# First token block of a PEER router: gates by accumulating indirect transfers instead of matmuls

## The chip, the cores and the metric
The kernel runs on one core of one Trainium2 chip. The metric is device time in microseconds (us) of one execution, the median of several. One execution was also run under the hardware profiler; the rows below come from that one. Two timings of this kernel that differ by less than about 0.2% can't be told apart.

## The reference
512 tokens of width 1024 pass through two layers. Each layer is a mixer (layer 0: pooling and retention; layer 1: a gated linear recurrence), a layer norm, a PEER block and a second layer norm. The change is in the PEER block, which both layers run with their own weights:

```python
q = (xt @ w_q).reshape(T, 8, 2, 128)                  # 8 heads, two half queries each
s = einsum('thpd,hpkd->thpk', q, sub_keys)            # 128 scores for each half
s_top, i_top = top_k(s, 16)
cand = s_top[:, :, 0, :, None] + s_top[:, :, 1, None, :]
best, pos = top_k(cand, 16)                           # 16 experts of 16384 for each head
eid = i_top[..., 0] * 128 + i_top[..., 1]             # at pos
gate = softmax(best)
act = gelu(einsum('td,thkd->thk', xt, u_tab[eid]))
out = einsum('thk,thkd->td', gate * act, v_tab[eid])
```

So every token uses 8 x 16 = 128 of 16384 experts, each with a gate.

## The kernel before
Tokens are cut into four blocks of 128 (`tb` 0 to 3). Blocks 0 to 2 (`TD` = 384 tokens) are computed **densely**: all 16384 experts are multiplied out for all 384 tokens, and a dense table of gates, nearly all zeros, is multiplied in between. Block 3 is computed **sparsely**: 256 indirect loads on POOL's queue (the engine is GpSimd) fetch the rows it needs.

The 16384 experts are 128 chunks of 128, in 32 groups of four (`NG` = 32, `NB` = 4). For one chunk `mm1` does 24 matmuls of 384 columns (three products of split float32 for each of 8 slices of the width), then Gelu; I call this a **lookahead block** where it is done early. `mm2` multiplies the gated result with the chunk of `peer_v` and adds it up in PSUM over all chunks. Weights pass through `stream`: a load on SP's queue into one of 5 `raw` buffers, ACT rounds it to `hi`, DVE (VectorE) subtracts to get `lo`; there are 6 `hi` and 6 `lo` buffers.

The **route** of a layer runs ahead of the experts:
- `route_topk`, first half: for each of four chunks `c` of the query projection (two heads each), 96 matmuls of 512 columns, then for each token block the scores against the keys on PE and the best 16 of 128 on DVE.
- `route_topk`, second half: for each token block (order 3, 0, 1, 2), all 8 heads at once: add the candidates, take the best 16, softmax, and `lookup`, which turns positions into the two key numbers of each expert. For blocks 0 to 2 the numbers and gates are transposed by PE into `kT`.
- `route_gates`: for every 8 dense tokens one **gate round**: DVE builds two one-hot tables `oh` and `og`, PE multiplies them in 16 matmuls of 128 columns in float16 (half of them on line 779, half on 780), ACT copies the product to `gbuf`. Every 32 tokens, `gbuf` (2 MB) is written to the DRAM tensor `gd`. There are 48 rounds a layer.

The route is a Python generator that yields an estimated cost at several places (`YC`, `Y2`, and constants). `peer` adds these up, and for each 2.8 units it emits one lookahead block. So there are 14 groups (`NLA`), 56 blocks, computed during the route and, all but two groups, spilled to DRAM `sp`. A scheduler then fixes the order on each engine; each engine runs its own in order.

In `experts`, SP loads the gates of a group (`gt` from `gd`) and, for the early groups, `ge` from `sp`; DVE multiplies; PE does `mm2` and the `mm1` of the other 18 groups. Beside it POOL fetches rows for block 3 (`gather_rounds`, line 832).

Of the kernel before, what the change touches and what calls it, by code (L numbers as in the profile page):

```python
# [20 lines left out]
P = 128  # L21
# [7 lines left out]
GS = 16384.0  # L29
NB = 4  # L30
NG = NE // NB
TD = 3 * P
NSD = TD // 32
NLA = 14
KEEP = 2
# [3 lines left out]
Y2 = 1.4  # L39
# [4 lines left out]
GW = 8  # L44
WINDOWS = (2, 4, 8, 16)
NEG = -3.0e38


class Kern:
# [547 lines left out]
    def peer(self, layer, xT, hs, out):  # L597
        nc, tc, io = self.nc, self.tc, self.io
        gd = self.dram.tile([NG, P, NSD, NB, 32], F32, name="gd%d" % layer, tag="gd%d" % layer)
        sp = self.dram.tile([NLA, P, NB, TD], F32, name="sp%d" % layer, tag="sp%d" % layer)  # L600
        with tc.tile_pool(name="pe", bufs=1) as pe:
            self.pe = pe
            self.eid = pe.tile([P, P], I32, name="eid", tag="eid")
            self.gate3 = pe.tile([P, P], F32, name="gate3", tag="gate3")
            self.x3 = pe.tile([P, D], F32, name="x3", tag="x3")
            g, b = self.load_ln(layer, 0)

            def norm(tb):
                self.layernorm(tb, hs[tb], g, b, xT)
                if tb == NTB - 1:  # L610
                    nc.scalar.copy(self.x3, hs[tb])
                    nc.scalar.mul(hs[tb], hs[tb], ALPHA)

            self.out_proj(io["c_w_out" if layer else "ab_w_out"], xT, hs, norm)
            self.kept = {}
            look = self.lookahead(layer, xT, sp)
            with tc.tile_pool(name="rk", bufs=1) as rk:
                kT = rk.tile([P, TD // GW, 4, GW], F16, name="kT", tag="kT")
# [4 lines left out]
                for gen in (self.route_topk(layer, xT, kT), self.route_gates(layer, kT, iot, gd)):  # L623
# [8 lines left out]
            self.experts(layer, xT, hs, gd, sp, lambda tb: self.layernorm(  # L632
                tb, hs[tb], g1, b1, None if layer else xT, out if layer else None))
        return xT
# [23 lines left out]
    def route_topk(self, layer, xT, kT):  # L658
        nc, tc, io = self.nc, self.tc, self.io
        with tc.tile_pool(name="rt", bufs=1) as rt, tc.tile_pool(name="rt2", bufs=2) as rt2, \  # L660
                tc.tile_pool(name="rs2", bufs=1) as rs2:
            i16 = rt.tile([P, 16], F16, name="i16", tag="i16")
# [7 lines left out]
            def sink_q(n, ps):  # L670
                q = rt2.tile([P, T], F32, name="qh", tag="qh", bufs=5)
                nc.scalar.copy(q, ps)
                qs.append(q)

# [25 lines left out]

            for tb in (3, 0, 1, 2):
                sv = stop[:, tb].rearrange("p (h two) s -> p h two s", two=2)
                s0, s1 = sv[:, :, 0, :], sv[:, :, 1, :]
                iv = itop[:, tb].rearrange("p (h two) s -> p h two s", two=2)
                i0, i1 = iv[:, :, 0, :], iv[:, :, 1, :]
                cand = rs2.tile([P, 8, 64], F32, name="cand", tag="cand")
                at = 0
                for a, b, m in ((0, 1, 16), (1, 4, 8), (4, 8, 4), (8, 16, 1)):
                    n = b - a
                    ov = cand[:, :, at:at + n * m].rearrange("p h (i j) -> p h i j", j=m)  # L710
                    nc.vector.tensor_tensor(ov, s0[:, :, a:b, None].broadcast_to([P, 8, n, m]),
                                            s1[:, :, None, 0:m].broadcast_to([P, 8, n, m]), ALU.add)
                    at += n * m
                best = rs2.tile([P, 8, 16], F32, name="best", tag="best")
                pos = rs2.tile([P, 8, 16], U32, name="pos", tag="pos")
                for h in range(8):
                    c2 = rs2.tile([P, 64], F32, name="c2", tag="c2")
                    cv = cand[:, h, :]
                    nc.vector.max(out=best[:, h, 0:8], in_=cv)
                    nc.vector.max_index(out=pos[:, h, 0:8], in_max=best[:, h, 0:8], in_values=cv)  # L720
                    nc.vector.match_replace(out=c2, in_to_replace=best[:, h, 0:8], in_values=cv, imm_value=NEG)
                    nc.vector.max(out=best[:, h, 8:16], in_=c2)
                    nc.vector.max_index(out=pos[:, h, 8:16], in_max=best[:, h, 8:16], in_values=c2)
                    yield 0.7
                if tb == 3:
                    gate = self.gate3.rearrange("p (h s) -> p h s", h=8)
                else:
                    gate = rs2.tile([P, 8, 16], F32, name="gate", tag="gate")
                nc.vector.tensor_tensor(gate, best, best[:, :, 0:1].broadcast_to([P, 8, 16]), ALU.subtract)
                nc.scalar.activation(gate, gate, AF.Exp)  # L730
                sm = rs2.tile([P, 8], F32, name="gsm", tag="gsm")
                nc.vector.tensor_reduce(sm, gate, AX.X, ALU.add)
                nc.vector.reciprocal(sm, sm)
                nc.vector.tensor_tensor(gate, gate, sm[:, :, None].broadcast_to([P, 8, 16]), ALU.mult)
                kk = yield from self.lookup(rs2, pos, i0, i1, thr, i16)
                if tb == 3:
                    ef = rs2.tile([P, P], F32, name="ef", tag="fi")
                    fl = "p h s -> p (h s)"
                    nc.vector.scalar_tensor_tensor(ef, kk[0].rearrange(fl), 128.0, kk[1].rearrange(fl),
                                                   ALU.mult, ALU.add)  # L740
                    nc.vector.tensor_copy(self.eid, ef)
                    continue
                tg = slice(tb * P // GW, (tb + 1) * P // GW)
                ghT, glT = kT[:, tg, 2, :], kT[:, tg, 3, :]
                pt = self.psC.tile([P, 512], F32, name="pC", tag="pC")
                for i, t in enumerate((kk[0], kk[1], gate)):
                    nc.tensor.transpose(pt[:, i * P:(i + 1) * P], t.rearrange("p h s -> p (h s)"), self.ident)
                nc.scalar.copy(kT[:, tg, 0:2, :].rearrange("p g i w -> p i g w"),
                               pt[:, 0:2 * P].rearrange("p (i g w) -> p i g w", i=2, w=GW))
                gs = rs2.tile([P, P // GW, GW], F32, name="gs", tag="gs")  # L750
                nc.scalar.mul(gs, pt[:, 2 * P:3 * P].rearrange("p (g w) -> p g w", w=GW), GS)
                nc.scalar.copy(ghT, gs)
                nc.vector.tensor_tensor(glT, gs, ghT, ALU.subtract)

    def route_gates(self, layer, kT, iot, gd):
# [3 lines left out]
        with tc.tile_pool(name="rg", bufs=2) as rg:  # L759
            b5 = [P, 2, Q, P, L]  # L760
            for s in range(NSD):
# [25 lines left out]
    def lookup(self, pool, pos, i0, i1, thr, i16):  # L787
        nc = self.nc
        sh, sx = [P, 8, 16], [P, 8, 16, 16]
        pf = pool.tile(sh, F32, name="pf", tag="pf")  # L790
        nc.vector.tensor_copy(pf, pos)
        m = pool.tile(sh, F32, name="m", tag="m")
        m2 = pool.tile(sh, F32, name="m2", tag="m2")
        mi = pool.tile(sh, U32, name="mi", tag="mi")
# [6 lines left out]
        yield 1.5  # L801
        d0 = pool.tile(sh, F16, name="d0", tag="d0")
# [3 lines left out]
        for src, cst, op, val, nm in ((pf, thr, ALU.is_ge, d0, "ka"), (mi, i16, ALU.is_equal, i1, "kb")):  # L806
            x = pool.tile(sx, F16, name="xp", tag="xp", bufs=2)
            nc.scalar.copy(x, src[:, :, :, None].broadcast_to(sx))
            nc.vector.tensor_tensor(x, x, cst[:, None, None, :].broadcast_to(sx), op)
            yield 2.0  # L810
            nc.vector.tensor_tensor(x, x, val[:, :, None, :].broadcast_to(sx), ALU.mult)
            yield 2.0
            t1 = pool.tile([P, 8, 16, 8], F16, name="t1", tag="t1")
            nc.vector.tensor_tensor(t1, x[:, :, :, 0:8], x[:, :, :, 8:16], ALU.add)
            t2 = pool.tile([P, 8, 16, 4], F16, name="t2", tag="t2")
            nc.vector.tensor_tensor(t2, t1[:, :, :, 0:4], t1[:, :, :, 4:8], ALU.add)
            t3 = pool.tile([P, 8, 16, 2], F16, name="t3", tag="t3")
            nc.vector.tensor_tensor(t3, t2[:, :, :, 0:2], t2[:, :, :, 2:4], ALU.add)
            k = pool.tile(sh, F32, name=nm, tag=nm)
            nc.vector.tensor_tensor(k, t3[:, :, :, 0], t3[:, :, :, 1], ALU.add)  # L820
            res.append(k)
            yield 1.0
# [32 lines left out]
    def experts(self, layer, xT, hs, gd, sp, norm):  # L855
        nc, tc, io = self.nc, self.tc, self.io
        with tc.tile_pool(name="ex", bufs=2) as ex, tc.tile_pool(name="ga", bufs=2) as ga:
# [19 lines left out]
            def front(i):  # L877
# [3 lines left out]
                if b == 0:  # L881
# [7 lines left out]
                    nc.sync.dma_start(out=gt, in_=gd[g])  # L889
# [95 lines left out]
def _shape_constants():  # L985
# [24 lines left out]
    c["ident"] = np.eye(P, dtype=f)  # L1010
    return c
# [57 lines left out]
```

## Time and profile before

| | |
|---|---|
| median of 3 runs | 2875.28 us (2873.82 to 2875.84) |
| the profiled execution's own time | 2876.77 us |
| its span in the profile | 2875.0 us |
| busy PE, DVE, ACT, POOL | 99%, 82%, 40%, 25% of the span |
| route of layer 0, first scores to last gate round | 190 to 553 us |
| first `mm2` of layer 0 | 573.89 us |
| DMA, read and written in HBM | 669.31 MB, 71.30 MB |

The span is what the profile's rows cover; the execution's own time is 1.8 us longer. PE is the matmul engine; an engine's busy share is an average over stages. Layer 1 repeats the PEER block of layer 0 some 1482 us later.

### The profile page before, as it was taken

Reading aid. Unit: us, or ns where it says so; the run is one execution under the profiler, and the core shown is the slowest. Engines: PE = TensorE matmul, PEld = TensorE weight load, DVE = VectorE, ACT = ScalarE, POOL = GpSimd, SP = SyncE. Lnnn points to the kernel's source line nnn. Section 1 sums busy time; section 2 is a strip of 40 time slices with the busy share of each in tenths; the row PEclk is TensorE's granted clock in tenths of the full one; section 3 lists DMA queues with packets and bytes.
Section 4 is the critical chain, followed back from the end, with each engine's and each line's share of the span. In section 5 each row is a group of like instructions: output and inputs, shape, how many; then the busy total and the mean of one; then the engine's idle time right before and its main releaser. Section 6 shows DMA issues by size and latency. Waiting matters only on the chain.

```text
span 2875.0 us, 42578 instructions
## 1 busy us (share of the span) xinstructions
PE 2858.8 (99%) x15832; PEld 2556.3 (89%) x15832; DVE 2369.7 (82%) x4482; ACT 1143.7 (40%) x1707; POOL 722.6 (25%) x539
## 2 busy tenths in 40 slices
PE   9999999999999999999999999999999999999998
PEld 7888999988898888888888889999888989889887
DVE  6779999788888888876797779999678888888786
ACT  3333565433333333334334333565433333333332
POOL 0000000145444455440000000000244454544440
PEclk9999999999999999999999999999999999999999
DMA  6223469999999999995322234479998999989982
GB/s 223 91 97 114 149 206 287 280 368 373 351 345 365 340 376 340 343 363 166 104 81 70 96 99 137 157 244 281 316 375 335 361 371 340 371 331 350 353 323 74
DMA packets 283792, 743.41 MB, mean 259 GB/s; under 512 B 21696, under 2 KB 120512, under 8 KB 283584
## 3 DMA queue, kind: packets, MB, share of 16 engines
q1 hardware_dynamic: 209856, 472.22, 47.2%
q0 software_dynamic: 73728, 268.47, 24.0%
q8 instruction: 124, 2.03, 0.3%
q14 instruction: 84, 0.69, 0.1%
HBM read 669.31 MB, written 71.30 MB: 258 GB/s over the span
## 4 chain that ended last, share of the span: by engine, by line
PE 93%; DVE 5%; DMA 1%; issue 1%; ACT 0%; POOL 0%; SPq 0%; DVEq 0%
PE pB L937 18%; PE pC L937 18%; PE pA L91 14%; PE pA L93 14%; PE pA L92 14%; PE pC L91 2%; PE pC L93 2%; PE pC L92 2%; PE pB L779 1%; PE pB L780 1%; DVE lo L76 1%; DVE oh L772 1%; DVE og L773 1%; PE pC L158 1%; DVE s L695 1%
## 5 line engine op out<-in xcount | busy, mean ns | idle before, releaser
L75 ACT CAST hi<-raw 128x1024 fp32r<-128x1024 f32 (+1 forms) x609 | 638.1, 1051 | 654.6 <-PE pA L92 412.5
L76 DVE TENSOR_TENSOR lo<-raw,hi 128x1024 fp32r<-128x1024 f32 (+1 forms) x609 | 736.4, 1216 | 178.8 <-ACT hi L75 170.1
L832 POOL DMA_INDIRECT row<-in_u,eid x256 | 388.1, 1516 | 1491.2 <-DVE av L842 581.2
L91 PE MATMUL pA<-xThi,hi 128*128 128x384 f32 (+2 forms) x2032 | 700.8, 345 | 2.4 <-ACT hi L75 2.4
L93 PE MATMUL pA<-xThi,lo 128*128 128x384 f32 (+2 forms) x2032 | 699.6, 344 | 0.0
L92 PE MATMUL pA<-xTlo,hi 128*128 128x384 f32 (+2 forms) x2032 | 697.3, 343 | 0.1
L91 PEld LDWEIGHTS pA<-xThi,hi 128*128 128x128 f32 x2032 | 382.0, 188 | 19.8 <-ACT hi L75 3.3
L92 PEld LDWEIGHTS pA<-xTlo,hi 128*128 128x128 f32 x2032 | 381.9, 188 | 17.0 <-DVE xTlo L76 0.4
L93 PEld LDWEIGHTS pA<-xThi,lo 128*128 128x128 f32 x2032 | 381.7, 188 | 14.3
L75 ACT CAST ch<-ge 128x384 fp32r<-128x384 f32 x256 | 131.4, 515 | 607.0 <-PE pC L937 483.8
L832 POOL DMA_INDIRECT row<-in_v,eid x256 | 327.6, 1280 | 158.6 <-DVE h L851 102.2
L851 DVE SCALAR_TENSOR_TENSOR h<-row,cf,h 128x1024 f32<-128x1024 f32 x256 | 327.7, 1280 | 0.9 <-DMA row<-in_v,eid 0.8
L842 DVE CUSTOM_DVE_ANT_0 row<-row,x 128x1024 f32<-128x1024 f32 x256 | 310.9, 1215 | 3.8 <-DMA row<-in_u,eid 3.8
L937 PE MATMUL pC<-hi,ch 128*128 128x512 f32 x768 | 300.0, 391 | 0.0
L937 PE MATMUL pB<-hi,cl 128*128 128x512 f32 x768 | 299.6, 390 | 0.4 <-DVE cl L76 0.3
L937 PE MATMUL pB<-lo,ch 128*128 128x512 f32 x768 | 299.9, 390 | 0.0
L937 PE MATMUL pB<-hi,ch 128*128 128x512 f32 x768 | 299.1, 389 | 0.7 <-ACT ch L75 0.7
L937 PE MATMUL pC<-hi,cl 128*128 128x512 f32 x768 | 299.5, 390 | 0.0
L937 PE MATMUL pC<-lo,ch 128*128 128x512 f32 x768 | 298.7, 389 | 0.0
L905 DVE TENSOR_TENSOR ge<-ge,gt 128x384 f32<-128x384 f32 x256 | 134.5, 551 | 157.3 <-DMA ge<-sp 146.9
L76 DVE TENSOR_TENSOR cl<-ge,ch 128x384 fp32r<-128x384 f32 x256 | 141.0, 551 | 62.5 <-ACT ch L75 61.9
L937 PEld LDWEIGHTS pB<-hi,cl 128*128 128x128 f32 x768 | 144.1, 188 | 32.1 <-DVE cl L76 1.6
(261 smaller groups left out, 4126.1 us busy)
## 6 DMA issues: line engine op xcount, KB each, us to landing
raw<-in_peer_ut SPq DMA_DIRECT2D x256, 512.0 KB, 4.9
raw<-in_peer_v SPq DMA_DIRECT2D x256, 512.0 KB, 6.9
gd<-gbuf SPq DMA_DIRECT2D x24, 2048.0 KB, 10.0
gt<-gd SPq DMA_DIRECT2D x64, 768.0 KB, 7.2
sp<-ge SPq DMA_DIRECT2D x24, 768.0 KB, 5.3
ge<-sp SPq DMA_DIRECT2D x24, 768.0 KB, 9.4
raw<-in_peer_w_q SPq DMA_DIRECT2D x32, 512.0 KB, 4.3
raw<-in_c_w_in SPq DMA_DIRECT2D x32, 512.0 KB, 3.9
```

The source lines that it names most:

```text
L75: self.nc.scalar.copy(hi, src)
L76: return self.nc.vector.tensor_tensor(lo, src, hi.bitcast(F32), ALU.subtract)
L91: nc.tensor.matmul(ps, ah, bh, start=(first and i == 0), stop=False)
L92: nc.tensor.matmul(ps, ah, bl, start=False, stop=False)
L93: nc.tensor.matmul(ps, al, bh, start=False, stop=(last and i == n - 1))
L158: nc.tensor.transpose(ps[:, i * P:(i + 1) * P], src[:, (q + i) * P:(q + i + 1) * P], self.ident)
L695: nc.vector.match_replace(out=s2, in_to_replace=mx[:, 0:8], in_values=sc, imm_value=NEG)
L832: nc.gpsimd.indirect_dma_start(out=t, out_offset=None, in_=io[name], in_offset=bass.IndirectOffsetOnAxis(ap=self.eid[:, j:j + 1], axis=0))
L842: nc.vector.tensor_tensor_reduce(ur, ur, x3, 1.0, 0.0, ALU.mult, ALU.add, av[:, k:k + 1])
L851: nc.vector.scalar_tensor_tensor(acc, vr, coefs[i // GQ][:, i % GQ:i % GQ + 1], acc, ALU.mult, ALU.add)
L905: nc.vector.tensor_tensor(gv, gv, gt[:, :, b, :], ALU.mult)
L937: nc.tensor.matmul(acc[hf], a[:, ts], b[:, hf * 512:(hf + 1) * 512], start=first and i == 0, stop=last and i == 2)
```

## The change
Block 0 no longer goes through the transposes and gate rounds. After the scores of token block 0 in each chunk, the two heads of that chunk choose their experts at once (`choose(0, c * 2, 2)`), and a new class `Scatter` computes, for each of the 32 (head, rank) columns, the address of each token's gate in a new DRAM tensor `gz`, and issues one indirect transfer per column that **adds** 128 gates of 4 bytes to it. `gz` is filled with zeros first, by 32 transfers of 256 KB on SP's queue. As two heads of a token may choose the same expert, each transfer of a head is made to wait for all 16 of the head before it. `gd` and `kT` lose block 0, so 32 gate rounds a layer are left of 48. In `experts`, `gt` is loaded in two pieces, from `gd` and from `gz`; the `gz` piece of the first two groups goes through POOL's queue. `Y2`, the cost put down for a gate round, goes from 1.4 to 2.0. The number of groups ahead stays 14. `choose` and `lookup` are the old code with the number of heads as an argument.

```diff
 NLA = 14
+NSZ = 4
-Y2 = 1.4
+Y2 = 2.0
+class Scatter:
+    def __init__(self, k, pool, layer):
...
+        self.dst = k.dram.tile([NG, P, NSZ, NB, 32], F32, name=self.name, tag=self.name)
+        z = pool.tile([P, NSZ * NB * 32], F32, name="zero", tag="zero")
+        nc.gpsimd.memset(z, 0.0)
+        for g in range(NG):
+            nc.sync.dma_start(out=self.dst[g].rearrange("p s b t -> p (s b t)"), in_=z)
+    def place(self, k, pool, c, k0, k1):
...
+        nc.vector.tensor_scalar(x, k1, 0.25, -0.375, ALU.mult, ALU.add)
+        nc.vector.tensor_scalar(x, x, RND, RND, ALU.add, ALU.subtract)
+        nc.vector.tensor_scalar(y, k0, float(row), self.pcol, ALU.mult, ALU.add)
+        nc.vector.scalar_tensor_tensor(y, k1, 32.0, y, ALU.mult, ALU.add)
+        nc.vector.scalar_tensor_tensor(y, x, float(P * row - 32 * NB), y, ALU.mult, ALU.add)
+        nc.vector.tensor_copy(idx, y)
+        flat = self.dst.rearrange("g p s b (t o) -> (g p s b t) o", o=1)
+        for h in range(2):
...
+            for j in range(h * 16, h * 16 + 16):
+                d = nc.gpsimd.indirect_dma_start(
+                    out=flat, out_offset=bass.IndirectOffsetOnAxis(ap=idx[:, j:j + 1], axis=0),
+                    in_=gate[:, j:j + 1], in_offset=None, compute_op=ALU.add).ins
+                for p in self.last:
+                    tc.add_manual_dep(d, p.name, LANDED, reason="adds of different heads may meet")
...
+            self.last = head
...
                     yield YC[c]
+                    if tb == 0:
+                        yield from choose(0, c * 2, 2)
+            for tb in (3, 1, 2):
+                yield from choose(tb, 0, 8)
...
-            for s in range(NSD):
+            for s in range(NSD - NSZ):
                 gbuf = rg.tile([P, P, 32], F32, name="gbuf", tag="gbuf")
...
-                    nc.sync.dma_start(out=gt, in_=gd[g])
+                    nc.sync.dma_start(out=gt[:, NSZ:], in_=gd[g])
+                    gz.read(nc.gpsimd if i < 2 * NB else nc.sync, gt[:, :NSZ], g)
```

Three places show how instructions move. The first is DVE's order while token blocks 0 and 1 of the first query chunk are ranked. Before, there is nothing but the ranking of scores (`stop`, `ix`, `s`; lines 693 to 697):

```order
L695 MATCH_REPLACE s_1702<-stop,pB 128x128
L693 MAX stop<-pB 128x8
L696 MAX stop<-s_1702 128x8
L694 MAX_INDEX ix<-stop,pB 128x8
L697 MAX_INDEX ix<-stop,s_1702 128x8
```

Of the changed kernel, the same place (ranking is now lines 806 to 810):

```order
L809 MAX stop<-s_1871 128x8
L750 MAX best<-c_1742 128x8
L810 MAX_INDEX ix<-stop,s_1871 128x8
L751 MAX_INDEX pos<-best,c_1742 128x8
L759 TENSOR_TENSOR gate_1405<-best 128x32
L806 MAX stop<-pB 128x8
L856 CAST pf<-pos 128x32
L807 MAX_INDEX ix<-stop,pB 128x8
L860 TENSOR_SCALAR m<-pf 128x32
L861 TENSOR_SCALAR m_1757<-pf 128x32
```

The choice of two heads stands between the rankings, in instructions a quarter as wide as those of an eight-head choice. The second place is POOL's order from the start of the route of layer 0 to the first row fetched for block 3 (`iot` and `i` are constant tables). Before:

```order
L944 MEMSET z 128x512
L620 ISA
L620 IOTA iot 128x256
L663 IOTA i_1417 128x16
L832 DMA row<-in_u,eid 128x1024 x9
```

Of the changed kernel:

```order
L1010 MEMSET z 128x512
L65 MEMSET zero 128x512
L674 ISA
L674 IOTA iot 128x256
L717 IOTA i_1462 128x16
L86 DMA gz_1415<-gate_1405,idx_1409 2097152x1 x32
L86 DMA gz_1415<-gate_1406,idx_1410 2097152x1 x32
L86 DMA gz_1415<-gate_1407,idx_1411 2097152x1 x32
L86 DMA gz_1415<-gate_1408,idx_1412 2097152x1 x32
L97 DMA gt<-gz_1415 128x512 x2
L897 DMA row<-in_u,eid 128x1024 x9
```

128 adding transfers and two gate loads now stand ahead of POOL's first row. The third place is SP's queue behind the layer norm's constants. Before:

```order
L179 DMA lnb<-in_ln_b 128x1024
L665 DMA thr<-in_thr 128x16
L678 DMA keys<-in_keysT 128x512
L81 DMA raw<-in_peer_w_q 128x1024
L678 DMA keys<-in_keysT 128x512
```

Of the changed kernel:

```order
L62 DMA pcol<-in_pcol 128x1
L67 DMA gz_1415<-zero 128x512 x32
L719 DMA thr<-in_thr 128x16
L791 DMA keys<-in_keysT 128x512
L134 DMA raw<-in_peer_w_q 128x1024 x2
L134 DMA raw<-in_peer_ut 128x1024
```

The zeros now stand ahead of the third load of the query projection's weights.

## Rows read from the trace of the kernel before

**Rows 1.** The page: busy us, share of the span, instructions of an engine
```profile
PE 2858.8 (99%) x15832; PEld 2556.3 (89%) x15832; DVE 2369.7 (82%) x4482; ACT 1143.7 (40%) x1707; POOL 722.6 (25%) x539
```

**Rows 2.** Waits of PE: who for whom, us in total, times, longest
```profile
PE pA L91 <- ACT hi L75: 2.4, 2, 1.9
...
PE pB L684 <- DVE s L695: 0.6, 2, 0.3
```

**Rows 3.** Timeline of PE among gate rounds: start, us, instruction
```profile
458.34 0.42 PE L91 MATMUL pA<-xThi,hi 128*128 128x384 f32 x1
...
464.69 0.42 PE L91 MATMUL pC<-xThi,hi 128*128 128x384 f32 x1
```

**Rows 4.** Timeline of PE among lookahead blocks alone
```profile
300.45 0.34 PE L91 MATMUL pC<-xThi,hi 128*128 128x384 f32 x1
...
304.62 0.34 PE L91 MATMUL pA<-xThi,hi 128*128 128x384 f32 x1
```

**Rows 5.** Timeline of PE around one transpose of chosen experts
```profile
350.38 0.27 PE L747 MATMUL pC<-c_ident,ka 128*128 128x128 f32 x1
...
350.62 0.42 PE L91 MATMUL pC<-xThi,hi 128*128 128x384 f32 x1
350.88 0.33 PE L92 MATMUL pC<-xTlo,hi 128*128 128x384 f32 x1
```

**Rows 6.** First and last scores of layer 0: ns min/median/max, starts
```profile
L684 PE MATMUL pB<-keys,qh x128: 269/275/378, 190.0 to 292.0; 128*128 128x128 f32 x128
```

**Rows 7.** Windows: DVE busy us (instructions), clock, DMA share, GB/s
```profile
293.00:403.00 110.00, 106.02 (x440) 1.00 0.47 157
```

**Rows 8.** Windows: PE, PEld, DVE, ACT, POOL busy us, clock, DMA
```profile
260.00:280.00 20.00, 20.00 (x106) 17.76 (x105) 17.26 (x77) 7.70 (x11) 0.00 (x0) 1.00 0.32 105
```

**Rows 9.** Timeline of DVE: small instructions of the choice of experts
```profile
306.84 0.17 DVE L803 COPY d<-itop 128x8 f16<-128x8 f16 x1
306.90 0.22 DVE L804 TENSOR_TENSOR d<-itop 128x120 f16<-128x120 f16 x1
...
314.72 0.18 DVE L733 RECIPROCAL gsm<-gsm 128x8 f32<-128x8 f32 x1
314.82 0.17 DVE L722 MAX8 best<-c 128x8 f32<-128x64 f32 x1
```

**Rows 10.** The one-hot tables: ns min/median/max, first and last start
```profile
L779 PE MATMUL pB<-og,oh x768: 217/218/235, 407.2 to 2035.6; 128*128 128x128 f16 x192
...
L772 DVE TENSOR_TENSOR oh<-iot,kT x96: 1214/1218/1226, 403.7 to 2030.7; 128x2048 f16<-128x2048 f16 x96
```

**Rows 11.** Softmax's table loads on ACT, 190 to 400 us
```profile
L730 ACT ACT_TABLE_LOAD x4 | 5.1, 1283 | 0.1
```

**Rows 12.** Timeline of POOL, a row fetched early in layer 1
```profile
2052.95 0.93 POOL L832 DMA_INDIRECT row<-in_u,eid  x1 [0.30 <-issue]
```

**Rows 13.** Indirect row loads: ns min/median/max, starts; and landing
```profile
L832 POOL DMA_INDIRECT row<-in_u,eid x256: 933/1679/1968, 565.6 to 2756.9; - x128
L832 POOL DMA_INDIRECT row<-in_v,eid x256: 932/1295/2147, 583.4 to 2790.6; - x128
...
DMA to landing us min/median/max: 4.6/8.3/12.2
```

**Rows 14.** Loads of gates: ns min/median/max, first and last issue
```profile
L889 SPq DMA_DIRECT2D gt<-gd x64: 326/327/877, 564.7 to 2785.9; - x64
```

**Rows 15.** Timeline of SP's issues at the end of layer 0's mixer
```profile
124.59 0.43 SPq L179 DMA_DIRECT2D lnb<-in_ln_b  x1
...
128.49 0.43 SPq L81 DMA_DIRECT2D raw<-in_peer_w_q  x1
```

**Rows 16.** DMA issues: count, KB each, median us to landing
```profile
gd<-gbuf SPq DMA_DIRECT2D x24, 2048.0 KB, 10.0
...
raw<-in_peer_w_q SPq DMA_DIRECT2D x32, 512.0 KB, 4.3
```

**Rows 17.** Timeline of ACT: first cast of a late load
```profile
161.21 1.05 ACT L75 CAST hi<-raw 128x1024 fp32r<-128x1024 f32 x1 [0.78 <-ACT xThi L163]
```

More of the change, by code (lines that the diff above doesn't have):

```diff
@@ L46, with read @@
 NEG = -3.0e38
+RND = 12582912.0
+LANDED = mybir.DependencyInfo(mybir.DependencyClass.Sync, mybir.DependencyReason.DATA)
+class Scatter:
+    def __init__(self, k, pool, layer):
+        nc, self.tc = k.nc, k.tc
+        self.name = "gz%d" % layer
+        self.last = []
+        self.gate = [k.pe.tile([P, 2, 16], F32, name="gate0", tag="gate0", bufs=4) for _ in range(4)]
+        self.idx = [k.pe.tile([P, 2 * 16], I32, name="idx0", tag="idx0", bufs=4) for _ in range(4)]
+        self.pcol = pool.tile([P, 1], F32, name="pcol", tag="pcol")
+        nc.sync.dma_start(out=self.pcol, in_=k.io["pcol"])
+        self.dst = k.dram.tile([NG, P, NSZ, NB, 32], F32, name=self.name, tag=self.name)
[4 more added lines that the diff above has]
+    def place(self, k, pool, c, k0, k1):
+        nc, tc = k.nc, k.tc
+        idx, gate = self.idx[c], self.gate[c].rearrange("p h s -> p (h s)")
+        x = pool.tile([P, P], F32, name="ix0", tag="fi")[:, :32]
+        y = pool.tile([P, P], F32, name="iy0", tag="fj")[:, :32]
+        nc.vector.tensor_scalar(x, k1, 0.25, -0.375, ALU.mult, ALU.add)
+        nc.vector.tensor_scalar(x, x, RND, RND, ALU.add, ALU.subtract)
+        row = NSZ * NB * 32
+        nc.vector.tensor_scalar(y, k0, float(row), self.pcol, ALU.mult, ALU.add)
[4 more added lines that the diff above has]
+        for h in range(2):
+            key = "%s.%d" % (self.name, c * 2 + h)
+            head = []
+            for j in range(h * 16, h * 16 + 16):
[4 more added lines that the diff above has]
+                    tc.add_manual_dep(d, p.name, LANDED, reason="adds of different heads may meet")
+                tc.declare_no_dep(d, group=key, reason="a head's sixteen experts differ")
+                tc.add_to_no_dep_group(key, d)
+                head.append(d)
+            self.last = head
+    def read(self, engine, out, g):
+        d = engine.dma_start(out=out, in_=self.dst[g]).ins
+        for p in self.last:
+            self.tc.add_manual_dep(d, p.name, LANDED, reason="all adds of the last head")
@@ L598, in peer @@
         nc, tc, io = self.nc, self.tc, self.io
-        gd = self.dram.tile([NG, P, NSD, NB, 32], F32, name="gd%d" % layer, tag="gd%d" % layer)
+        gd = self.dram.tile([NG, P, NSD - NSZ, NB, 32], F32, name="gd%d" % layer, tag="gd%d" % layer)
         sp = self.dram.tile([NLA, P, NB, TD], F32, name="sp%d" % layer, tag="sp%d" % layer)
@@ L617, in peer @@
             with tc.tile_pool(name="rk", bufs=1) as rk:
-                kT = rk.tile([P, TD // GW, 4, GW], F16, name="kT", tag="kT")
+                gz = Scatter(self, rk, layer)
+                kT = rk.tile([P, (TD - P) // GW, 4, GW], F16, name="kT", tag="kT")
                 iot = rk.tile([P, P, 2], F16, name="iot", tag="iot")
@@ L622, in peer @@
                 credit = CREDIT0
-                for gen in (self.route_topk(layer, xT, kT), self.route_gates(layer, kT, iot, gd)):
+                for gen in (self.route_topk(layer, xT, kT, gz), self.route_gates(layer, kT, iot, gd)):
                     for cost in gen:
@@ L631, in peer @@
             g1, b1 = self.load_ln(layer, 1)
-            self.experts(layer, xT, hs, gd, sp, lambda tb: self.layernorm(
+            self.experts(layer, xT, hs, gd, gz, sp, lambda tb: self.layernorm(
                 tb, hs[tb], g1, b1, None if layer else xT, out if layer else None))
@@ L656, in lookahead, with route_topk @@
                 yield
-    def route_topk(self, layer, xT, kT):
+    def route_topk(self, layer, xT, kT, gz):
         nc, tc, io = self.nc, self.tc, self.io
@@ L699, in route_topk @@
                     yield YC[c]
[L701 to L753, printed above, removed]
@@ L788, in lookup @@
         nc = self.nc
-        sh, sx = [P, 8, 16], [P, 8, 16, 16]
-        pf = pool.tile(sh, F32, name="pf", tag="pf")
+        n = pos.shape[1]
+        part = n / 8.0
+        sh, sx = [P, 8, 16], [P, n, 16, 16]
+        pf = pool.tile(sh, F32, name="pf", tag="pf")[:, :n]
         nc.vector.tensor_copy(pf, pos)
-        m = pool.tile(sh, F32, name="m", tag="m")
-        m2 = pool.tile(sh, F32, name="m2", tag="m2")
-        mi = pool.tile(sh, U32, name="mi", tag="mi")
+        m = pool.tile(sh, F32, name="m", tag="m")[:, :n]
+        m2 = pool.tile(sh, F32, name="m2", tag="m2")[:, :n]
+        mi = pool.tile(sh, U32, name="mi", tag="mi")[:, :n]
         nc.vector.tensor_scalar(m, pf, 56.0, 3.0, ALU.is_lt, ALU.mult)
@@ L800, in lookup @@
         nc.vector.tensor_tensor(mi, mi, pos, ALU.bitwise_and)
-        yield 1.5
-        d0 = pool.tile(sh, F16, name="d0", tag="d0")
+        yield 1.5 * part
+        d0 = pool.tile(sh, F16, name="d0", tag="d0")[:, :n]
         nc.vector.tensor_copy(d0[:, :, 0:1], i0[:, :, 0:1])
@@ L853, in gather_rounds, with experts @@
             yield
-    def experts(self, layer, xT, hs, gd, sp, norm):
+    def experts(self, layer, xT, hs, gd, gz, sp, norm):
         nc, tc, io = self.nc, self.tc, self.io
@@ L1010, in _shape_constants @@
     c["ident"] = np.eye(P, dtype=f)
+    c["pcol"] = (s // 32 * 128 + s % 32)[:, None].astype(f)
     return c
```

74 lines of the change are left out of this document (66 added, 8 removed).

## The prediction
> **What bounds the kernel now.** I read the page first: PE is busy 2858.8 of 2875.0 us, 99%; DVE, ACT and POOL 82%, 40% and 25% [rows 1]. PE's waits name few real stops: 2.4 us in all for ACT's `hi` and 0.6 us for DVE's ranked scores [rows 2]. So PE is the bound, its queue is in order, and only two things change the time: matmul work taken from PE, and new waits of PE. I therefore read next what a gate round costs PE, and then how much room the engines have that must do the replaced work. DVE decides there. The first scores are multiplied at 190.0 us, the last at 292.0 [rows 6]; the first one-hot table of the gate rounds starts at 403.7, the first gate matmul at 407.2 [rows 10]. From 293 to 403 DVE is busy 106.02 of 110.00 us [rows 7], and from 260 to 280, the loosest stretch of the ranking, 17.26 of 20 [rows 8]. So before the gate rounds DVE is nearly a second bound.
>
> **Gate rounds removed.** Among the gate rounds PE repeats a pattern of 24 lookahead matmuls and two rounds (32 gate matmuls); its start is at 458.34 and again at 464.69 [rows 3], 6.35 us. The 24 matmuls alone take 304.62 - 300.45 = 4.17 us [rows 4]. Two rounds thus cost PE 2.18 us, one 1.09. Sixteen a layer go, 32 in all: 32 x 1.09 = 34.9 us. The lookahead blocks between them don't go: 14 groups, 56 blocks, are made before as after, and by the order the same count of them stands ahead of the first gate round. `Y2` only spaces the rounds wider. DVE saves two tables of 1.22 us for each round [rows 10], but there PE is the one that is waited for, so this counts nothing. **-35 us.**
>
> **Transposes removed.** Three of a block take from 350.38 to 350.62, and the matmul behind them 0.26 instead of 0.17 us, since it is the first of another form [rows 5]: 0.33 us for one block a layer, **-0.7** for two. The same 0.09 us is paid at each change between scores and lookahead matmuls. With the choices in between, the order cuts PE's row into 31 such stretches a layer in the score chunks instead of 22; 9 x 0.09 x 2 is **+2** rounded up.
>
> **DVE's added work.** One choice of 8 heads has 29 instructions that are as wide as the heads (the rest is per head and unchanged in number). As four choices of 2 heads there are 116, so 87 more, each a quarter as wide. What the extra ones cost is the fixed part: a `COPY` of 128x8 starts at 306.84 and the next instruction at 306.90, a `RECIPROCAL` of 128x8 at 314.72 and the next at 314.82 [rows 9]; at 0.06 to 0.10 us, 5 to 9. `place` adds 6 instructions four times, 24 at 0.10: 2.4. Together about 8, with a range of 7.6 to 11. Against this the free time is 4.0 us from 293 to 403 [rows 7] and 2.7 from 260 to 280 [rows 8]; the rest of the ranking is fuller. Also, three more softmax stretches a layer each change ACT's table twice, 1.283 us a load [rows 11]; if DVE finds nothing to do meanwhile, up to 5 us more are lost. So DVE needs 8 to 13 us and has 6.7: it is 1.3 to 6.3 us late a layer at the first gate round. PE then waits, as its order has no other work there and nothing is in hand: two `oh` and one `og` of 1.22 us each from 403.7 end where the first matmul starts, 407.2 [rows 10]. I take 4, being nearer the case where other rankings fill the table loads only in part. **+8**, with 0 as the lower bound (the ranking may have smaller gaps outside the two stretches that serve as well) and +26 as the upper (13 a layer and no gap serves).
>
> [...]
>
> **The adding transfers.** POOL has nothing to do from 190 to 403 us: its column in the window is 0.00 [rows 8]. No transfer that adds is in the trace; the nearest is a row load by indices. Its issue takes 0.93 with 0.30 ahead, 1.23 us [rows 12], at most 2.147 + 0.30 = 2.45 [rows 13]; a landing takes 8.3 us, 12.2 at most [rows 13]. Heads go one behind the other: 16 x 1.23 + 8.3 = 28 us a head, 8 heads 224. The first pair of heads is chosen some 20 us after 190, so the end is at about 435. The first gates are fetched at 564.7 [rows 14]; 17.4 less of gate rounds, plus the stall, puts that at 551. About 116 us are spare, and I cost it at nothing. The row loads of block 3 wait behind it on POOL, but they too begin only at 565.6 [rows 13]. The slow end stands among the rivals.
>
> **Zeros.** 32 transfers of 256 KB, 8.4 MB, stand on SP's queue between the layer norm's constants (124.59) and the third load of `w_q` (128.49) [rows 15]. The nearest is `gd`, 2 MB in 10.0 us [rows 16]: 40 us for the fill, so it ends at about 165, and the load 4.3 us later, at 169. ACT casts the load behind it at 161.21 [rows 17]. If loads queue strictly behind the fill, that is 8 us late a layer, +16 in all; if the fill leaves bandwidth, nothing. Pieces are 2 KB here and 512 bytes in `gd`, so I take the faster end, **0**.
>
> **In `experts`** the gates come in two loads where there was one: SP has 62 more issues a layer at 0.33 us [rows 14], 20 us in 900, and the bytes are the same. PE's loads are ahead by 5 `raw` buffers, so nothing.
>
> **Sum.** -35 - 0.7 + 2 + 8 = -25.7. The profiled execution took 2876.8, its span 2875.0; this one would take 2851. The median is 1.5 lower, 2875.3 - 25.7 = 2849.6, **2850**.
>
> **Rivals.**
> *DVE has no room at all.* Its 13 us a layer all become waits of PE: -35 - 0.7 + 2 + 26 = -8, 2868. For it: DVE at 96% in the window [rows 7]. Against: the small pieces fill gaps that exist, and the table loads of one pair can lie behind the ranking of the next block.
>
> *The adding transfers are late* (slower). If each issue costs 2.45 us, as the row loads at worst do while DVE is busy, a head takes 39.2 + 8.3 = 47.5 and eight take 380: the end is at 590 instead of 551, 39 late a layer. PE has no gates then and waits in `experts`: 2850 + 78 = 2928. It cancels the gain at about 13 us late a layer, an end at 564, 44 us a head, an issue of 2.25 us. For it: DVE is never idle while POOL issues, and row loads in `experts`, beside a busy DVE, have a median of 1.30 to 1.68 [rows 13]. Against: at that median (1.68 + 0.30) a head takes 40, eight 320, the end is 530, still in time; it takes the worst row for all 128. [...]
>
> *The zeros delay the query weights:* +16, 2866, by the terms above.
>
> *The rounds are not what PE pays for.* If, with fewer rounds, lookahead blocks merely wait for weights instead, the gain is lost: 2875. For it: little; ACT's and DVE's tables per us fall. Against: blocks alone run at 4.17 us without a wait [rows 4].
>
> **How the numbers follow.** The forecast with 0 to 6.3 us of stall a layer (2842 to 2855) has 0.72; DVE without room 0.10; the transfers late 0.08; the zeros 0.06; nothing gained 0.04. The range 2841 to 2868 takes in the first two and the zeros. About 0.2%, 6 us, is what a measurement of this kernel can tell from no change. Faster by more: the first three of them, 0.88, less a little for a full DVE and late transfers together: 0.86. Within 0.2%: nothing gained and the transfers a little late, 0.06. Slower: the transfers late, 0.08.
>
> **What will show it.** Of one-hot tables there should be 64 of each kind instead of 96, and of gate matmuls 1024 instead of 1536 (two lines of 768 before), with PE's busy time down by about 34. The first table of the gate rounds against the last wait of PE before it shows DVE's term; a wait of PE for DVE or ACT of 1 to 6 us a layer is expected there. POOL's last adding transfer should be issued near 430 us, and no wait of PE for a gate load should follow. The third `w_q` load should be cast by 162. The forecast is wrong by tens of us if the first `mm2` waits for POOL, and by some 16 if the projection waits for weights.

## The result and the profile after

The changed kernel takes 2840.87 us (median of 4, 2840.38 to 2841.03) against 2874.66 (median of 4) for the kernel before: 33.8 us less, ratio 0.9882, interval 0.9865 to 0.9899. The forecast was 2850, in a range from 2841: right in direction, 9 us too high, and 0.13 us outside the range. The profiled execution took 2840.96 with a span of 2838.9; its span is 36.1 shorter than that of before, whose profiled execution lay 2.1 above its median.

The page, the first line, which answers to [rows 1]:

```profile
PE 2822.2 (99%) x15314; PEld 2526.6 (89%) x15314; DVE 2311.6 (81%) x4638; ACT 1129.5 (40%) x1667; POOL 1197.5 (42%) x801
```

PE is still the bound, with 36.6 us less to do. The first scores, the first gate matmul (half of the gate matmuls have this line) and the first `mm2`, by line (ns min/median/max, first and last start):

```profile
L797 PE MATMUL pB<-keys,qh x256: 270/275/377, 189.3 to 1782.6; 128*128 128x128 f32 x128
...
L842 PE MATMUL pB<-og,oh x512: 217/218/233, 408.4 to 1994.2; 128*128 128x128 f16 x171
...
L1003 PE MATMUL pB<-hi,ch x768: 387/389/396, 557.3 to 2827.1; 128*128 128x512 f32 x192
```

These starts cut the route of layer 0 in two, and both parts are read in the same way for layer 1:

| us | before | after | |
|---|---|---|---|
| first scores to first gate matmul | 217.2 | 219.1 | +1.9 (layer 1: +1.7) |
| first gate matmul to first `mm2` | 166.7 | 148.9 | -17.8 (layer 1: -19.1) |
| all the rest, both layers | | | -2.8 |

Before, the first `mm2` has this line; the starts of the scores and gate matmuls are in [rows 6] and [rows 10]:

```profile
L937 PE MATMUL pB<-hi,ch x768: 387/389/501, 573.9 to 2862.5; 128*128 128x512 f32 x192
```

In layer 1 the three starts are 1672.7, 1889.9 and 2057.4 us before, and 1655.8, 1874.6 and 2023.1 after.

The whole gain lies where the gate rounds are. Ahead of them PE lost a little, and its waits (us in total, times, longest) say to whom:

```profile
PE pC L780 <- DVE kb L885: 1.5, 2, 0.7
...
PE pC L780 <- DVE ka L885: 1.2, 2, 0.6
...
PE pB L842 <- DVE og L836: 0.7, 2, 0.4
...
PE pB L797 <- ACT qh L726: 0.6, 2, 0.3
```

The first three are the choice of block 1 and the first gate table, late by DVE, each of them once a layer; [rows 2] had no such line. To see why the loss is small, compare DVE from the first scores to the first table, before and after. Columns: us, then busy (instructions) of PE, PEld, DVE, ACT, POOL, the clock, DMA share, GB/s. Before:

```profile
190.00:403.60 213.60, 213.20 (x1184) 200.57 (x1183) 204.93 (x936) 98.21 (x135) 0.00 (x0) 1.00 0.41 138
```

After:

```profile
189.30:404.80 215.50, 213.57 (x1184) 200.50 (x1183) 210.56 (x1046) 106.37 (x147) 157.07 (x91) 1.00 0.57 137
```

DVE has 110 instructions more and is busy 5.6 us longer, 0.05 us for each. It was idle 8.7 us and is idle 4.9, so 3.7 of the 5.6 went into gaps and 1.9 is what the route grew. Its own waits around that stretch are these (the longest, 11.8, ended at 188.3, ahead of it), and none is for the softmax on ACT:

```profile
DVE lo L129 <- ACT hi L128: 13.6, 2, 11.8
DVE xp L874 <- ACT xp L873: 1.4, 1, 1.4
```

The adding transfers took longer than forecast. Their row (ns min/median/max, first and last start):

```profile
L86 POOL DMA_INDIRECT gz<-gate,idx x256: 1538/1622/2917, 209.4 to 1962.6; - x128
```

POOL's timeline at the last transfer of layer 0 and the first gate load:

```profile
501.52 1.97 POOL L86 DMA_INDIRECT gz<-gate,idx  x1 [0.30 <-issue]
539.23 1.20 POOL L97 DMA_DIRECT2D gt<-gz  x2 [35.74 <-DMA raw<-in_peer_v]
```

From 209.4 to 501.5 there are 127 steps of 2.30 us on average, the waits between heads included; the forecast's 224 us for 128 are 1.75 a step. An issue takes 1.82 on average where the forecast had 0.93, and between two heads POOL waits 2.2 to 6.2 us where it had 8.3. So the transfers end at 503.5, not 435, and 36 us are spare, not 116.

The zeros cost no time that the trace shows. SP's timeline has their issue and that of the next `w_q` loads:

```profile
125.28 24.84 SPq L67 DMA_DIRECT2D gz<-zero  x32
...
151.61 0.84 SPq L134 DMA_DIRECT2D raw<-in_peer_w_q  x2
```

ACT's timeline has the cast that answers to [rows 17]:

```profile
160.52 1.05 ACT L128 CAST hi<-raw 128x1024 fp32r<-128x1024 f32 x1 [0.78 <-ACT xThi L216]
```

And the window of the fill (columns as above):

```profile
125.00:150.00 25.00, 25.00 (x112) 20.71 (x111) 13.29 (x19) 5.80 (x6) 0.75 (x2) 1.00 1.00 348
```

The fill runs at 348 GB/s and is over by some 153 us (335 GB/s from 151 to 152, 111 from 153 to 154); the cast starts at the same distance from the first scores as before (28.8 us) and waits for ACT's own work. But the load that it needs was issued at 151.61 instead of 128.49 [rows 15]; if it landed 4.3 us later [rows 16], some 5 us were spare (an estimate; its landing is not in the trace).

### The profile page after: what moved, and what is told of

Its sections match the earlier page's. It is cut to its first block, busy times and chain, and to the rows that moved or that the text cites. A ratio compares the mean times of both kernels' runs of the same rounds, so it can differ in the third digit from the quotient of the medians.

```text
span 2838.9 us, 42026 instructions
## 1 busy us (share of the span) xinstructions
PE 2822.2 (99%) x15314; PEld 2526.6 (89%) x15314; DVE 2311.6 (81%) x4638; ACT 1129.5 (40%) x1667; POOL 1197.5 (42%) x801
## 4 chain that ended last, share of the span: by engine, by line
PE 90%; DVE 8%; DMA 1%; issue 1%; ACT 0%; SPq 0%; DVEq 0%; ACTq 0%
PE pC L1003 18%; PE pB L1003 18%; PE pA L144 14%; PE pA L146 14%; PE pA L145 14%; DVE lo L129 2%; PE pC L144 2%; PE pC L146 2%; PE pC L145 2%; PE pB L842 1%; PE pB L843 1%; PE pB L797 1%; PE pC L211 1%; DVE xp L874 0%; DVE xp L876 0%
## 5 line engine op out<-in xcount | busy, mean ns | idle before, releaser
L897 POOL DMA_INDIRECT row<-in_u,eid x256 | 398.6, 1557 | 615.7 <-DVE av L907 591.2
L86 POOL DMA_INDIRECT gz<-gate,idx x256 | 464.4, 1814 | 287.2 <-DVE stop L809 168.5
```

Of the source, the lines that this page charges most:

```text
L86: d = nc.gpsimd.indirect_dma_start(out=flat, out_offset=bass.IndirectOffsetOnAxis(ap=idx[:, j:j + 1], axis=0), in_=gate[:, j:j + 1], in_of ...
L897: nc.gpsimd.indirect_dma_start(out=t, out_offset=None, in_=io[name], in_offset=bass.IndirectOffsetOnAxis(ap=self.eid[:, j:j + 1], axis=0))
```

## The experiments

Two theories stand against each other. By the first, each gate round was worth about 1.1 us of PE, and the new work of DVE and POOL fits beside PE but for some 2 us a layer. By the second, part of the gain came from elsewhere (fewer bytes, an earlier end of the gate writes), and DVE's work cost nothing. Each run has the kernel before beside it on the same chip, with a median of 2874.6 to 2875.4. The runs were made on several chips, so each ratio is to the kernel before on its own chip.

**The rounds put back.**

```diff
-            for s in range(NSD - NSZ):
+            for n in range(NSD):
+                s = n % (NSD - NSZ)
...
+                if n < NSZ:
+                    continue
                 nc.sync.dma_start(out=gd[:, :, s]...
```

> The changed kernel with 16 more gate rounds a layer, computed from another block's numbers and thrown away; nothing else differs, so the result is the same and only PE, DVE and ACT do the removed work again. If a round costs PE the 1.09 us that the trace of before gave, 32 of them bring 35 us back: 2876 (2873 to 2879). If part of the gain came from elsewhere (fewer bytes of gates written, an earlier end of the gate writes), it stays below 2870.

Measured: 2919.39, far above both. PE's waits show where:

```profile
PE pB L1006 <- ACT ch L128: 32.9, 2, 16.6
PE pB L843 <- DVE og L837: 6.1, 6, 2.4
```

At the first `mm2` of each layer PE stood 16.5 us. In the order of PE's instructions, no lookahead block is left behind the last gate round there (the changed kernel has 6.9): the spacing of 2.0 used them all up among 48 rounds, and the last gates had still to be written and loaded. So the time of this run doesn't give the price of a round by itself; the next one takes the old spacing, `Y2 = 1.4`.

> The 16 extra gate rounds a layer, thrown away as before, now with the old spacing (cost 1.4 for a round instead of 2.0), so that lookahead blocks are left behind the last round. If the 33 us that PE waited in front of the first mm2 of each layer in the run with the spacing of 2.0 came from the cover used up there, and a round costs PE 1.09 us: 2876 (2873 to 2879), 43 less than that run. If the extra rounds themselves cost 2.4 us each: 2919 again.

Measured: 2877.0 (ratio to before 1.0008, 0.9999 to 1.0018), 36 above the changed kernel. Its first gate matmul and first `mm2`:

```profile
L843 PE MATMUL pB<-og,oh x768: 217/218/233, 408.3 to 2037.9; 128*128 128x128 f16 x192
...
L1006 PE MATMUL pB<-hi,ch x768: 387/389/397, 574.9 to 2862.9; 128*128 128x512 f32 x192
```

166.6 us instead of 148.9: 17.7 for 16 rounds, 1.11 each. Here 5.0 blocks are left behind the last round, as before, and PE does not wait ahead of the first `mm2`. The bytes of gates written are those of the changed kernel, so they are not the gain. The first theory holds: the rounds are.

**The spacing alone** (`Y2 = 1.4` with 32 rounds).

> The changed kernel with the old spacing of its gate rounds (cost 1.4 instead of 2.0): 14.6 lookahead blocks between the rounds and 13 behind them instead of 20.7 and 6.9; the matmul work is the same. If the spacing matters only while the cover behind the last round runs out, as it did with 48 rounds: 2841 (2839.5 to 2842.5). If denser rounds make DVE's tables late (2 tables a round against half a lookahead block): slower, up to 2850.

Measured: 2841.54 (ratio 0.9885, 0.9869 to 0.9902), as the first case had it. With blocks left over behind the last round, 6.9 in the changed kernel and 13 here, the spacing moves nothing that can be told (0.7 us).

**Block 0 chooses nothing.** The yields stay, so PE's order is the same. The adding transfers go with the choice.

```diff
-                        yield from choose(0, c * 2, 2)
+                        for cost in (0.7, 0.7, 0.375, 0.5, 0.5, 0.25, 0.5, 0.5, 0.25):
+                            yield cost
```

> Block 0 chooses no experts and adds no gates (its gates stay zero, so this is left out of the output); PE's order stays the same. DVE loses some 25 us of work a layer before the first gate round. If the changed kernel's stops of PE in the route (about 2 us a layer more than before) are DVE being late, they go: 2837 (2835 to 2838.5). If they come from something else, it stays at 2841.

Measured: 2835.52 (ratio 0.9864, 0.9848 to 0.9881), 5.3 below the changed kernel. First scores and first gate matmul:

```profile
L797 PE MATMUL pB<-keys,qh x256: 270/275/377, 188.9 to 1779.0; 128*128 128x128 f32 x128
...
L843 PE MATMUL pB<-og,oh x512: 217/218/233, 405.0 to 1988.4; 128*128 128x128 f16 x171
```

216.1 us. The window up to the first gate matmul (columns as above), here and then before:

```profile
188.90:404.90 216.00, 216.00 (x1201) 203.44 (x1200) 192.56 (x846) 92.96 (x129) 0.00 (x0) 1.00 0.43 143
```

```profile
190.00:407.20 217.20, 216.80 (x1204) 203.99 (x1203) 208.46 (x940) 99.65 (x137) 0.00 (x0) 1.00 0.42 142
```

PE is never idle in this run, so this is its own pace with the changed order: 31 stretches of either kind, 16 of them scores, where before had 22 and 11. Before took 217.2, of which 0.3 were the transposes. So the more frequent change between scores and lookahead matmuls costs nothing that shows, and DVE being late (ACT's `qh`, some 0.3, included) costs 3.0 a layer after and about 0.8 before: the change added 2.2 a layer. As idle time of PE the traces show 2.3 and 2.0 of the 3.0 and 0.4 of the 0.8. The rest lies in matmuls that run longer, and what lengthens them is not shown.

**The transfers left out.**

```diff
-                d = nc.gpsimd.indirect_dma_start(
...
+                continue
```

> The choice stays, the 128 adding transfers a layer are left out (block 0's gates stay zero). If the transfers are hidden altogether: 2841 within 1 us. [...]

Measured: 2840.34 (ratio 0.9879, 0.9863 to 0.9896), within that 1 us. While they are in time, the transfers take nothing from DVE or PE that can be told apart (0.5 us).

**More small instructions on DVE.**

```diff
+        for _ in range(24):
+            nc.vector.tensor_scalar(x, k1, 0.25, -0.375, ALU.mult, ALU.add)
```

> Each of the four address computations a layer repeats its first instruction (128x32) 24 times more: 96 small DVE instructions a layer, 6 to 9 us by 0.06 to 0.10 us each. If DVE's free time is used up, as the forecast had it, all of it becomes waits of PE: 12 to 18 us, 2853 to 2859. If the 4.9 us a layer in which DVE is still idle in that stretch can serve: 2 to 9 us, 2843 to 2850.

Measured: 2849.07 (ratio 0.9912, 0.9896 to 0.9929), 8.2 above, at the upper end of the second case. The window of DVE, to the first table:

```profile
189.20:408.40 219.20, 215.11 (x1180) 201.47 (x1180) 217.21 (x1142) 106.68 (x147) 150.33 (x87) 0.99 0.56 137
```

96 instructions more are 6.65 us more of DVE, 0.069 each, inside the 0.06 to 0.10 of the forecast. Idle time fell from 4.9 to 2.0 and this stretch grew by 3.7; up to the first gate matmul it is 3.8 more, in layer 1 5.0. Of some 13 us added in both layers 8.2 are paid; the rest lies in gaps. PE's longest stop is now another one, for a `lo` that DVE makes late:

```profile
PE pC L148 <- DVE lo L131: 5.4, 2, 2.9
```

**All eight heads at the old place.**

```diff
-                    if tb == 0:
-                        yield from choose(0, c * 2, 2)
-            for tb in (3, 1, 2):
+            for tb in (3, 0, 1, 2):
```

> Block 0 chooses all 8 heads at once at its old place, behind block 3, and its 128 adding transfers a layer start there, at about 350 us instead of 209. At the measured 2.3 us from one transfer to the next they end at about 645, the first mm2 needs them at 557, so PE waits some 90 to 105 us a layer: 3020 to 3050, with the stretch from the first scores to the first gate round about 2 us a layer shorter. If POOL is faster when DVE has few small instructions (1.84 us, its floor): end at 605, about 2950. At the forecast's 1.23 us: end at 575, 2875 to 2885.

Measured: 3050.5 (ratio 1.0611, 1.0590 to 1.0632), the upper end of the first case. PE's waits have one new line:

```profile
PE pA L144 <- ACT ge L699: 210.1, 2, 105.2
```

POOL's timeline has the last transfers of layer 0 and the gate loads behind them:

```profile
640.54 1.54 POOL L86 DMA_INDIRECT gz<-gate,idx  x1 [0.30 <-issue]
642.38 1.54 POOL L86 DMA_INDIRECT gz<-gate,idx  x1 [0.30 <-issue]
646.51 1.20 POOL L97 DMA_DIRECT2D gt<-gz  x2 [2.59 <-issue]
```

The rival "the adding transfers are late" is real, at this place. The first scores and the first gate matmul:

```profile
L797 PE MATMUL pB<-keys,qh x256: 270/275/377, 189.1 to 1861.8; 128*128 128x128 f32 x128
...
L840 PE MATMUL pB<-og,oh x512: 217/218/233, 406.0 to 2096.1; 128*128 128x128 f16 x171
```

216.9 us, 2.2 less than after: the DVE term once more, by undoing it (the additional switches go with it, which showed no cost above).

**Four heads at a time**, behind the second and fourth chunk.

```diff
-                    if tb == 0:
-                        yield from choose(0, c * 2, 2)
+                    if tb == 0 and c % 2:
+                        yield from choose(0, c * 2 - 2, 4)
```

> Block 0 chooses 4 heads at a time, behind the second and the fourth query chunk, instead of 2 heads behind each. 58 wide DVE instructions and 12 address instructions a layer less, at the measured 0.05 us each 3.5 us: PE's stops in the route shrink by 1 to 2 us a layer, 2837 to 2839. The transfers start some 25 us later and end near 530, gates are read at 539; if they are late after all, PE waits at the first mm2 and it is slower than 2841 by as much.

Measured: 2860.2 (ratio 0.9951, 0.9935 to 0.9968), slower than two heads. The profiled execution, at 2856.3, was the fastest of the four. The adds start at 241.6 instead of 209.4, run at 2.40 us a step, and end too late, by their row and POOL's timeline:

```profile
L86 POOL DMA_INDIRECT gz<-gate,idx x256: 1539/1826/4242, 241.6 to 2017.7; - x128
...
545.90 1.54 POOL L86 DMA_INDIRECT gz<-gate,idx  x1 [0.30 <-issue]
549.94 1.21 POOL L97 DMA_DIRECT2D gt<-gz  x2 [2.50 <-issue]
```

PE's waits have the price (us in total, times, longest):

```profile
PE pA L144 <- ACT ge L699: 12.9, 2, 6.5
PE pB L797 <- DVE ix L810: 3.8, 2, 1.9
```

The gates are asked for at 549.9, 11 us later than in the changed kernel, and PE stands 6.5 us a layer. The route to the first gate round gained 0.6 in layer 0 and 0.3 in layer 1, less than the 1 to 2 expected: PE now stops for the `ix` of a ranking, as the second line shows. Starting the transfers 32 us later costs more than the saved instructions bring.

**One lookahead block earlier** (`YC[3]` 4.7 instead of 4.0).

> The cost put down for a ranking in the last query chunk goes from 4.0 to 4.7, so one lookahead block a layer moves from behind the last gate round to ahead of block 3's choice. If PE's stops at the transposes and the first gate round are DVE being late by up to 2 us, 4.2 us more of PE work there cover it: 2837 (2836 to 2839). If the stops only move to another place: 2841.

Measured: 2837.86 (ratio 0.9871, 0.9855 to 0.9888), the first case. The stops for `ka`, `kb` and `og` are gone; new ones come ahead of the first `mm2`, where one block less is left:

```profile
PE pA L144 <- issue: 1.8, 1, 1.8
...
PE pA L144 <- ACT ge L699: 1.0, 1, 1.0
```

So the rounds were set closer too (`Y2 = 1.8`), and then one more block was moved (`YC[1]` 0.7, `Y2 = 1.7`).

> One lookahead block a layer ahead of block 3's choice, as in the run with 4.7, and the gate rounds at a cost of 1.8, so that 8 blocks instead of 5.9 are left behind the last round. If the 1 to 2 us a layer that PE waited for the first gates in that run came from cover that had become too short, and the stops at the transposes stay covered: 2835.5 (2834.5 to 2836.5). If the stop for the first gates has another cause: 2838.

> As the run before it, with one more lookahead block in the second query chunk (cost 0.7 for a ranking instead of 0) and rounds at a cost of 1.7. If the stops of PE in the score chunks (some 1 us a layer, at 230 and 292 us) are DVE or ACT being late by less than a block: 2834 (2833 to 2835.5). If they come from the change between two kinds of matmuls at ACT, no gain over the run before it: 2835.5.

Measured: 2837.45 (ratio 0.9869, 0.9853 to 0.9886) and 2838.19 (0.9870, 0.9853 to 0.9886). The time of the first missed its 2835.5 and lies nearer to 2838, the case of another cause; it can't be told from the time with 4.7 alone. By the trace the stops ahead of the first `mm2` are gone, as the 2835.5 supposed. In that run, from the first scores to the first `mm2` 365.9 and 365.5 us against 368.0 and 367.4, and all that PE waits for in the route is

```profile
PE pB L797 <- ACT qh L726: 0.5, 2, 0.4
PE pB L797 <- DVE s L808: 0.4, 2, 0.2
```

This version is 3.4 us below the changed kernel, with runs (2836.77 to 2838.69) that don't overlap its runs, though on another chip; that is 0.12%, less than the 0.2% that a measurement of this kernel can tell, but the stops that it removes are gone from the trace. The second brought nothing more and missed both of its numbers (2834 and 2835.5): two stops of 0.1 to 0.3 us a layer remain in the score chunks, at other places, so one block more doesn't cover them. What causes them stays open.

**No writes of the dense gates.**

```diff
+                for g in range(NG):
+                    for u in range(2):
+                        nc.gpsimd.dma_start(out=gd[g][:, u * 4:u * 4 + 4]..., in_=gz.z)
...
-                nc.sync.dma_start(out=gd[:, :, s]...
```

> The dense gates are left out: gd is filled with zeros once by 64 transfers on POOL's queue ahead of the adds, and the 2 MB writes among the gate rounds are gone, while DVE and PE do the same work there. The last three heads of adding transfers took 1.96 to 2.05 us an issue beside the gate rounds (DMA share 0.95, DVE in 1.2 us instructions) and the second and third 1.62 to 1.66. If the load on the DMA engines is what lengthens POOL's issue, it falls to 1.55 to 1.7 there and the adds end some 10 us earlier, if they start at 209. If DVE's long instructions are, it stays at 1.95 to 2.05. The time: within 3 us of 2841 by either.

Measured: 2934.61 (ratio 1.0208, 1.0179 to 1.0238), missed by 90 us, for a reason that tests another rival: the fill is now three times as large, 25 MB. ACT's timeline at the first late load:

```profile
204.15 1.05 ACT L129 CAST hi<-raw 128x1024 fp32r<-128x1024 f32 x1 [44.81 <-DMA raw<-in_peer_w_q]
205.10 0.29 ACT L223 ACTIVATE sd<-mv,epst 128x1 f32<-128x1 f32 x1
```

The window of that wait, the DMA engines full at 361 GB/s and PE busy for 14 of 40 us:

```profile
150.00:190.00 40.00, 14.15 (x71) 11.54 (x69) 10.26 (x19) 2.44 (x5) 18.33 (x34) 0.74 1.02 361
```

A cast waits 44.8 us for `w_q` behind the zeros, the layer norm's `sd` waits behind the cast on ACT, DVE behind that, and PE stands 43 us in one layer and 40 in the other. Two thirds of these zeros stand on POOL's queue and not ahead of the load on SP's; with them SP's own 32 took 54 us to issue instead of 25, by SP's timeline:

```profile
124.92 54.45 SPq L68 DMA_DIRECT2D gz<-zero  x32
```

So the rival "the zeros delay the query weights" is real at 25 MB; at 8.4 MB it is not reached. On POOL's issues the run answers as meant. Beside the gate rounds, changed kernel:

```profile
420.00:503.00 83.00, 82.77 (x690) 79.22 (x688) 66.54 (x57) 41.43 (x72) 63.85 (x32) 1.00 0.95 256
```

and without the writes:

```profile
420.00:503.00 83.00, 81.71 (x613) 79.10 (x613) 74.15 (x119) 43.93 (x71) 67.77 (x34) 1.00 0.66 166
503.00:560.00 57.00, 56.84 (x475) 54.21 (x474) 45.39 (x39) 28.44 (x49) 33.10 (x16) 1.00 0.50 121
```

The first gate round of this run is at 452.7, so only its second window lies wholly beside gate rounds. POOL's busy time by its count is 2.00, 1.99 and 2.07 us an issue with DMA shares of 0.95, 0.66 and 0.50: the load on the DMA engines is not what makes an issue long.

## Why the forecast was 9 us too high

Two terms of the sum failed, both put too high: the switches (+2, measured at nothing) and DVE's added work (+8, measured at 4.4). With DVE's stall at nothing the sum is 2841.6, the low end of the range. The measured time lies below it although 4.4 us of stall are in it, so the DVE term alone does not carry the miss.

- *Gate rounds removed, -35:* right. -17.8 and -19.1 a layer up to the first `mm2`, 1.11 a round by putting them back, against 1.09.
- *Transposes, -0.7; more switches, +2:* the switches were wrong. The matmul behind a switch is 0.09 late, but the last one of the short form gives up its place 0.08 earlier, as the timeline of [rows 5] already held: three transposes take 0.24, and from start to start 0.11, 0.10 and 0.03. Without DVE's stops the route runs at 216.1, switches and all. Off by 2. The two transposes that [rows 5] leaves out:

```profile
350.49 0.27 PE L747 MATMUL pC<-c_ident,kb 128*128 128x128 f32 x1
350.59 0.27 PE L747 MATMUL pC<-c_ident,gate 128*128 128x128 f32 x1
```

- *DVE's added work, +8:* the mechanism was right, PE stops for DVE ahead of the first gate round, but the term was 4.4 (2.2 a layer, by leaving the choice out and by undoing it). Three parts of its working failed. The 110 instructions took 5.6 us, not 8, as one is followed at 0.05 us on average and not at 0.06 to 0.10; at the 0.069 of the added ones, the 24 of `place` are 1.7 of it and one that comes of the splitting costs 0.046 (an estimate from these two). The waits for ACT's table loads, up to 5 us, did not come at all: DVE has other work meanwhile, and from 189 to 405 it was busy for 97 to 100% of each of the first 14 loads and 89% of the 15th. (Three stretches with two loads of 1.283 are 7.7, so the 5 was not their sum either.) And the stall is not what is needed less what is free: by the measured 5.6 and 8.7 there would be none. Only 3.7 of the 8.7 us lay where they could serve. That the term came as near as it did is in part luck: the need was put too high, and all the free time was taken off it. Off by 3.6.
- *Adding transfers, 0:* the cost was right and its working was not. A step is 2.30 us, not 1.75, so the spare time is 36 us and not 116. The row loads at their best gave an end at 435; their median beside a busy DVE, which stands with the rival, gave 530, and 503.5 was measured. The rival stood much nearer than its chance of 0.08 said: a start 32 us later makes it true.
- *Zeros, 0, and the loads in `experts`, 0:* right. The fill ran at 348 GB/s instead of 210, and `experts` took 809.3 and 807.2 us from first to last `mm2` against 809.5 and 808.3. (Of the 62 issues that the forecast counts in `experts`, 32 are the zeros; 30 are loads.)

Switches, DVE and rounds make 6.2 of the 9 (2, 3.6 and 0.6), and 0.6 is the median of before, which was lower beside this kernel. Some 2 us stay open. Of these the traces show 0.7 ahead of the first scores, 0.7 behind the last `mm2` and 0.3 in `experts` of layer 0. The start of the first scores varies from 188.9 (no choice) to 189.6 (four heads) over kernels whose work up to there is the same, so the -0.7 there may be chance. The other two I did not settle. Layer 1 of before has a stop at its first `mm2` that the changed kernel doesn't have:

```profile
PE pB L937 <- ACT ch L75: 0.7, 1, 0.7
PE pB L937 <- DVE cl L76: 0.3, 1, 0.3
```

There layer 1 of before is 0.9 longer than its layer 0 ahead of the first `mm2`, and 1.1 longer than the changed kernel behind it. Together that is about the 2.1 us by which this execution lay above its median; whether other executions have the stop can't be seen.

## What to carry to other kernels

Where an engine is nearly full, add up the distances from one start to the next and not its instructions' lengths, and ask where its free time lies: here 8.7 us were free, 5.6 were needed, and PE still waited for 2. Ask too whether the engine can fill a wait with other work: here DVE was busy for at least 89% of each of ACT's 15 table loads in the route of layer 0. Price a new kind of transfer by how its neighbours run beside the same busy engines and not by their best, and ask how much later it may start: here a start 32 us later decided between -34 and -15. Work made ahead covers two places, in front of a consumer that is late and behind the last producer. A spacing that is free with 7 blocks left costs 16 us a layer when none is left.

## What was not expected of the hardware

An adding transfer of 128 pieces of 4 bytes took POOL 1.54 us an issue with all other engines idle (560 to 640 us in the eight-head run) and about 2.0 beside the gate rounds, with 0.30 of idle time ahead of nearly each in both; the row loads here took 0.93 at best. Among the 128 of layer 0, the 60 issues below 1.6 us had on average 0.37 us of long `TENSOR_TENSOR` instructions of DVE (`lo`, `oh`, `og` and some `xp`, 1.2 us each) beside them, and the 22 above 2.1 us 1.82. That is 24% and 76% of the issue. Short DVE instructions did not do it: at 209 to 310 us DVE was busy 97% of the time, mostly with them, and 34 of 48 issues stayed below 1.6 us. The long ones go along with issues that are 0.4 to 0.9 us longer on average (1.54 us below 1.6, 1.91 from there to 2.1, 2.39 above); what in them would lengthen an issue is not shown. That is read from the traces of these runs; that the load on the DMA engines is not the cause was tried, the rest is argued.
